# Two chains of the delta rule: the order of emission charges more for the three DVE steps of a chunk, in three of four pairs of heads

## The chip, the cores and the metric

One core of a Trainium2 chip. The metric is the device time of one execution in microseconds. An execution runs five engines with a queue each: PE (TensorE, matmuls; its weight loads are listed as PEld), DVE (VectorE), ACT (ScalarE), POOL (GpSimd) and SP (SyncE, which issues DMAs here). Each engine takes its queue in order, and an instruction waits on semaphores for the results of others.

## The reference

One layer of a hybrid encoder for a prompt of 2048 rows and a sample of 32, with 1024 columns, cut to what matters here:

```python
hp = layer_norm(x_prompt, ln0_g, ln0_b)
qa, ka, va, za, qkv_b, zb, a_b, b_b, gate_a, gate_b = split_projection(x @ w_in)
oa = chunk_band_attention(qa, ka, va, rel_bias)          # branch A, 8 heads of 64
c = silu(causal_conv(xp, conv_w, t))                     # branch B, 8 heads of 64
ob, s_new = gated_delta_rule(qb, kb, vb, g, beta, s_prev)
mix = sigmoid(gate_a) * ya + sigmoid(gate_b) * yb
y = layer_norm(ALPHA * x + mix @ w_out, ln_g, ln_b)
```

The delta rule works in chunks of 64 rows. Within a chunk everything can be prepared ahead (a triangular system per chunk and head); between chunks a state of 64 x 64 per head is handed on, which is a chain:

```python
def step(s, blk_in):
    q_c, k_c, u_c, w_c, gc_c, qk_c = blk_in
    v_new = u_c - w_c @ s
    o_c = (q_c * exp(gc_c)) @ s + qk_c @ v_new
    s = s * exp(g_last) + k_dec.T @ v_new
    return s, o_c
```

## The kernel before

The prompt is worked in two halves of 1024 rows. In each half come the input projection (jobs of 128 output columns, three passes of fp16 matmuls over 8 slices of the depth, into the PSUM tile `pj`), branch B (`phase_b`: convolution, gates, triangular systems, chains), then branch A (`phase_a`: scores, softmax, values). After both halves come the merge of the branches and the output projection. The jobs of the projection feed the branches, and those of the two merge gates feed nothing before the end and serve as filling: `all_jobs` lists them, with six gate jobs (`TAIL`) between branch B's jobs and branch A's.

The heads of branch B go in four pairs (`NP`), and a pair's 16 chunks of a half in two blocks of 8. A block's way is: `system` forms the chunk matrices (tiles `k_bd`, `qk_bd`, `p_c`), `solve` and `substitute` solve the triangular systems on DVE (31 pairs of `sys_t` and `sys_u`), `inverse` turns the result into `u_bd`, and `chain` runs through the chunks. Two banks (`x_banks = places(2)`) allow two chains at a time. In the second half the sample makes one more block, whose four chunks are the four pairs. Each chunk of a chain has three matmuls on PE into the tile `x`, each followed by a step on DVE that the next matmul needs:

- `x<-state,k_bd`, then DVE's `r` (a scalar_tensor_tensor)
- `x<-r,u_bd`, then DVE's `vn` (a tensor_scalar)
- `x<-vn,kd_bd`, then DVE's `state` (a scalar_tensor_tensor), for the next chunk

Two more matmuls per chunk, `o<-state,q_bd` and `o<-vn,qk_bd`, give the output, which ACT copies into `v_t`; `tail` scales and stores it.

The order of all queues is made by a planner in the program itself. Every piece of work is a generator (a `Stream`) with a clock of its own; `Flow.run` always resumes the stream whose clock is lowest, and each instruction that it emits moves its clock, and that of its engine, by a price (`Engine.price`, `Flow.spend`). For an instruction of DVE that reads PSUM the price is 0.125 us and 1/960 us per element, and 0.2 us more for coming from another engine (`HOP`); a matmul of fp32 into 64 columns has 128/600 us. The prices set the order of emission alone; on the chip nothing but queues and semaphores decides when something runs. The lines that charge:

```python
t = s.clock + (HOP_SAME if s.last == key else HOP)
t = max(t, self.busy.get(key, 0.0)) + cost
self.busy[key] = s.clock = t
```

All instructions are issued through one wrapper, line 259 of the kernel before (261 of the one after), so rows are told apart by their tiles.

Of the kernel before, what the change touches and what calls it, by code (L numbers as in the profile page):

```python
# [29 lines left out]
NP = NH // 2  # L30
# [18 lines left out]
NPAR, NSIDE = 4, 3  # L49
HEAD, TAIL = [2, 3], [6, 6]  # L50
AHEAD = 100.0
SPREAD = 20.0
HOP_PE, HOP, HOP_SAME = 0.1, 0.2, 0.12

# [213 lines left out]
def trunk(ctx: ExitStack, tc: tile.TileContext, x_p, x_s, cache_k, cache_v, st_conv, st_gdn,  # L268
# [4 lines left out]
    flow = Flow()  # L273
# [6 lines left out]
    def dma(dst, src, eng=nc.sync):  # L280

        eng.dma_start(dst, src)  # L282
        size = 2 if dst.dtype == F16 else 4
        n = size
        for k in dst.shape:
            n *= k

        n = max(n, n // (size * dst.shape[-1]) * 768)
        return flow.transfer("SP" if eng is nc.sync else "S", n)
# [153 lines left out]
    def spread():  # L443

        for h in range(NH):
            dma(ext_dram[h][:], ext_row[h:h + 1, :].to_broadcast([P, 768]))
            yield flow.cur.clock + SPREAD

# [327 lines left out]
    def phase_b(half):  # L776
# [518 lines left out]
        def outputs(m, x, os_, vc=None, end=None):  # L1295


            PE.matmul(os_, m, x, start=vc is None, stop=vc is not None)
            yield
            if vc is not None:  # L1300
                S.copy(out=vc, in_=os_)
                if end:
                    end.done()

        def chain(some):
            for k in some:
                yield k.ready
                xn = yield from x_banks.take()
                sc, v_t = k.sc, k.v_t
                xs, ys, ds_ = (xb[xn][:, i * HD:(i + 1) * HD] for i in range(3))  # L1310
                os_ = ob_[xn][:, 0:HD]
                for c in range(k.nch):
                    st = k.state[c]
                    vc = v_t[:, c if k.p is None else c % 4 * 2 + c // 4, :]
                    PE.matmul(xs, k.kb[:, c, :], st, start=True, stop=True)
                    yield
                    r = bp.tile([P, HD], F32, tag=f"r{xn}", bufs=2, name="r")
                    V.scalar_tensor_tensor(out=r[:], in0=xs, scalar=k.negc[:, c:c + 1], in1=vc, op0=ALU.mult, op1=ALU.add)
                    yield
                    PE.matmul(ys, k.ub[:, c, :], r[:], start=True, stop=True)  # L1320
                    flow.start(outputs(k.qb[:, c, :], st, os_))
                    yield
                    vn = bp.tile([P, HD], F32, tag=f"vn{xn}", bufs=2, name="vn")
                    V.tensor_scalar(out=vn[:], in0=ys, scalar1=sc[:, 1, c:c + 1], scalar2=None, op0=ALU.mult)
                    yield
                    PE.matmul(ds_, k.kdb[:, c, :], vn[:], start=True, stop=True)
                    flow.start(outputs(k.qkb[:, c, :], vn[:], os_, vc, k.out if c == k.nch - 1 else None))
                    V.scalar_tensor_tensor(out=st, in0=st, scalar=sc[:, 3, c:c + 1], in1=ds_, op0=ALU.mult, op1=ALU.add)
                    yield
                yield k.out  # L1330
                x_banks.back(xn)
                par_slots.back(k.par)
                side_slots.back(k.sn)
                u_slots.back(k.un)
                flow.start(tail(k))
# [84 lines left out]
        for some in blocks + ([[sample]] if last else []):  # L1420
            flow.start(chain(some))
# [795 lines left out]
    for half in range(2):  # L2217
# [12 lines left out]
        if half == 0:  # L2230
            flow.start(build_h(1, ap, 4), flow.cur.clock + AHEAD)
        if half == 0:
# [62 lines left out]
```

## Time and profile before

| | us |
|---|---|
| median of 3 runs | 2121.21 |
| lowest and highest run | 2118.57, 2124.31 |
| the profiled execution | 2124.96 |
| its span, first to last instruction | 2123.1 |
| PE busy in the span | 1994.4 |
| DVE busy | 1534.2 |
| ACT busy | 978.7 |
| POOL busy | 634.3 |

The span is what the rows below lie in; the time of an execution also has what lies around it. Busy time of PE counts a matmul from its start to a modelled end, so that matmuls which follow each other overlap in the records. Idle time is put down to what released the instruction behind it.

### The profile page before, as it was taken

The page shows a single profiled execution, that of the slowest core. Times are in us where ns is not written, and L with a number is a line of the kernel's source. Part 1 is how long each engine was busy: PE and PEld are TensorE (multiplying, and loading weights), DVE is VectorE, ACT ScalarE, POOL GpSimd, SP SyncE. Part 2 cuts the span into 40 slices and gives each one's busy share as a digit, 9 for nine tenths or more (in the row PEclk, how much of TensorE's full clock was granted, in tenths as well). Part 3 has the DMA queues.
Part 4 walks back from the last instruction along what each step waited for, and adds up shares of the span by engine and source line. Part 5 has one row for each costly group of instructions (what it writes and reads, how often), then busy time and mean ns, then how long its engine had stood idle before and what let it go on. Part 6 is the DMA issues. An engine that isn't in the chain of part 4 may idle for free. (4 is left out here: it accounts for less than half of the span.)

```text
span 2123.1 us, 41363 instructions
## 1 busy us (share of the span) xinstructions
PE 1994.4 (94%) x15098; PEld 1422.5 (67%) x15098; DVE 1534.2 (72%) x4660; ACT 978.7 (46%) x2098; POOL 634.3 (30%) x708
## 2 busy tenths in 40 slices
PE   4999898999999999999899999999999988999998
PEld 4454665666465656666666676767776777988896
DVE  7689989884277768779898987347657667766676
ACT  5655544443465667564444443346656652111110
POOL 6243333232322122333233232310110223443343
PEclk9999999899999999999999999999999999999999
DMA  3223232222423233222223233332322435443331
GB/s 120 75 84 102 76 88 78 67 79 82 122 67 120 82 93 99 70 73 76 58 70 94 62 86 85 99 100 72 92 77 67 138 120 191 128 123 103 116 107 61
DMA packets 197719, 196.49 MB, mean 93 GB/s; under 512 B 79622, under 2 KB 147570, under 8 KB 197516
## 3 DMA queue, kind: packets, MB, share of 16 engines
q1 hardware_dynamic: 197516, 193.85, 30.9%
q8 instruction: 119, 1.95, 0.4%
q14 instruction: 84, 0.69, 0.1%
HBM read 135.91 MB, written 50.53 MB: 88 GB/s over the span
## 5 line engine op out<-in xcount | busy, mean ns | idle before, releaser
L259 PE MATMUL pj<-hi,whi 128*128 128x512 f16 (+2 forms) x1992 | 650.7, 342 | 8.6 <-POOL whi L259 3.0
L259 PE MATMUL pj<-hi,wlo 128*128 128x512 f16 (+2 forms) x1952 | 640.8, 341 | 0.4 <-POOL wlo L259 0.4
L259 PEld LDWEIGHTS <-whi 128*128 128x128 f16 x3984 | 416.0, 106 | 217.5 <-issue 11.2
L259 PE MATMUL pj<-lo,whi 128*128 128x512 f16 (+2 forms) x1992 | 461.9, 340 | 0.0
L259 POOL TENSOR_TENSOR wlo<-wraw,whi 128x512 f16<-128x512 f32 x192 | 228.6, 1193 | 630.1 <-ACT whi L259 345.1
L259 PEld LDWEIGHTS <-wlo 128*128 128x128 f16 x1952 | 205.5, 105 | 108.5 <-issue 8.9
L259 ACT CAST mh<-sg 128x256 fp32r<-128x256 f32 x64 | 25.9, 407 | 276.1 <-DVE sg L259 276.0
L259 DVE TENSOR_TENSOR sys_u<-sys_u,sys_t 128x60 f32<-128x60 f32 (+24 forms) x527 | 135.7, 258 | 18.2
L259 PE MATMUL a<-ghi,whi 128*128 128x256 f32 (+1 forms) x512 | 134.8, 293 | 7.1 <-DVE sg L259 6.8
L259 ACT ACTIVATE wraw<-wraw,w_scale 128x1024 f32<-128x1024 f32 (+1 forms) x98 | 111.4, 1137 | 59.2 <-DVE w_scale L259 57.1
L259 ACT CAST ph<-b 128x512 f16<-128x512 f32 (+2 forms) x224 | 92.6, 422 | 92.7 <-PE b L259 86.1
L259 PE MATMUL a<-ghi,wlo 128*128 128x256 f32 (+1 forms) x512 | 131.9, 287 | 0.0
L259 ACT CAST whi<-wraw 128x512 f16<-128x512 f32 (+1 forms) x196 | 119.4, 611 | 27.1 <-PE pj L259 24.2
L259 DVE TENSOR_TENSOR pl<-b,ph 128x512 f16<-128x512 f32 (+2 forms) x224 | 107.6, 484 | 28.9 <-ACT ph L259 28.0
L259 DVE TENSOR_TENSOR sys_t<-sys_u,sys_p 128x54 f32<-128x54 f32 (+21 forms) x459 | 123.6, 269 | 4.0
L259 ACT ACTIVATE sb<-sb,mx,unit 128x640 f32<-128x640 f32 (+4 forms) x128 | 109.0, 852 | 25.5 <-DVE mx L259 25.1
L259 DVE SCALAR_TENSOR_TENSOR acc<-raw,cwT,acc 128x512 f32<-128x512 f32 x144 | 113.2, 786 | 8.4 <-ACT acc L259 7.4
L259 POOL TENSOR_TENSOR w_scale<-w_scale,mhalf 128x1 f32<-128x1 f32 x49 | 31.0, 633 | 288.0 <-DVE w_scale L259 230.1
L259 PEld LDWEIGHTS a<-ghi,whi 128*128 128x128 f32 x512 | 99.3, 194 | 8.8 <-DVE sg L259 7.9
L259 PE MATMUL b<-ident,sb 128*128 128x128 f32 x560 | 98.8, 276 | 2.9 <-ACT tmp L259 0.6
L259 ACT COPY v_t<-o 128x64 f32<-128x64 f32 x132 | 27.5, 209 | 158.3 <-PE o L259 121.5
L259 PEld LDWEIGHTS a<-ghi,wlo 128*128 128x128 f32 x512 | 98.9, 193 | 0.4 <-DVE wlo L259 0.2
(350 smaller groups left out, 4238.9 us busy)
## 6 DMA issues: line engine op xcount, KB each, us to landing
wraw<-in_w_in SPq DMA_DIRECT2D x192, 256.0 KB
sg<-sig SPq DMA_DIRECT2D x112, 128.0 KB
sig<-sig SPq DMA_DIRECT2D x44, 256.0 KB
sys_p<-sol_p SPq DMA_DIRECT2D x17, 512.0 KB
x<-in_x_p SPq DMA_DIRECT2D x16, 512.0 KB
xt<-in_x_p SPq DMA_DIRECT2D x16, 512.0 KB
out_y_p<-xt SPq DMA_DIRECT2D x16, 512.0 KB
glo<-g SPq DMA_DIRECT2D x14, 512.0 KB
```

Source lines behind the costliest of these rows:

```text
L259: r = f(*a, **k)
```

## The change

A constant is added, and in `chain` the clock of the stream is moved on by it after each of the three DVE steps, for pairs 0, 1 and 2 (`k.p in range(NP - 1)`); for pair 3 and for the sample (`k.p` is `None`) it is 0. The clock of DVE is not moved, only that of the chain: other streams may emit their work in the time between.

```diff
 AHEAD = 100.0
+
+SLACK = 0.4
...
                 sc, v_t = k.sc, k.v_t
+                slack = SLACK if k.p in range(NP - 1) else 0.0
...
                     V.scalar_tensor_tensor(out=r[:], in0=xs, scalar=k.negc[:, c:c + 1], in1=vc, op0=ALU.mult, op1=ALU.add)
+                    flow.cur.clock += slack
                     yield
...
                     V.tensor_scalar(out=vn[:], in0=ys, scalar1=sc[:, 1, c:c + 1], scalar2=None, op0=ALU.mult)
+                    flow.cur.clock += slack
                     yield
...
                     V.scalar_tensor_tensor(out=st, in0=st, scalar=sc[:, 3, c:c + 1], in1=ds_, op0=ALU.mult, op1=ALU.add)
+                    flow.cur.clock += slack
                     yield
```

The instructions are the same in number on every engine. Their order differs from the first chain on, at 209 us of the trace before. Two places on PE and one on DVE show how.

PE, first half, third chunk of pair 0's first block, from the matmul that takes r to the one that takes vn. `pj` rows are projections, `LDWEIGHTS` rows the loads of their weights. Before:

```order
L259 MATMUL x<-r,u_bd_629 128x64
L259 LDWEIGHTS whi
L259 MATMUL pj<-lo_151,whi 128x512
L259 MATMUL o<-state,q_bd_617 128x64
L259 LDWEIGHTS whi
L259 MATMUL pj<-lo_151,whi 128x512
L259 MATMUL x<-vn,kd_bd_623 128x64
```

Now:

```order
L261 MATMUL x<-r,u_bd_629 128x64
L261 LDWEIGHTS whi
L261 MATMUL pj<-hi_152,whi 128x512
L261 MATMUL o<-state,q_bd_617 128x64
L261 LDWEIGHTS wlo
L261 MATMUL pj<-hi_152,wlo 128x512
L261 LDWEIGHTS whi
L261 MATMUL pj<-hi_152,whi 128x512
L261 LDWEIGHTS wlo
L261 MATMUL pj<-hi_152,wlo 128x512
L261 MATMUL x<-vn,kd_bd_623 128x64
```

Between the two chain matmuls stand four projections where there were two.

PE, second half, fifth chunk of pair 0's first block, from the matmul that takes vn to the next chunk's first. `b<-qk,k_bd` rows are the chunk matrices of a later block. Before:

```order
L259 MATMUL x<-vn,kd_bd_10329 128x64
L259 MATMUL b<-qk_11407,k_bd_10313 128x128
L259 LDWEIGHTS wlo
L259 MATMUL pj<-hi_9644,wlo 128x512
L259 MATMUL o<-vn,qk_bd_10315 128x64
L259 MATMUL x<-state,k_bd_10307 128x64
```

Now:

```order
L261 MATMUL x<-vn,kd_bd_10298 128x64
L261 MATMUL b<-qk_11407,k_bd_10282 128x128
L261 LDWEIGHTS whi
L261 MATMUL pj<-hi_9940,whi 128x272
L261 MATMUL o<-vn,qk_bd_10284 128x64
L261 MATMUL b<-qk_11407,k_bd_10282 128x128
L261 LDWEIGHTS wlo
L261 MATMUL pj<-hi_9940,wlo 128x272
L261 MATMUL x<-state,k_bd_10276 128x64
```

One projection and one matmul of a chunk matrix have come between, and the place now falls among projections of 272 columns.

DVE, first half, the third chunk again, from r to state. `v_t` and `sys` rows belong to the preparation of later blocks. Before:

```order
L259 SCALAR_TENSOR_TENSOR r<-x,negc,v_t_654 128x64
L259 SCALAR_TENSOR_TENSOR qk_2258<-e,acc 128x512
L259 TENSOR_TENSOR v_t_656<-b,sc 64x2x2x64
L259 TENSOR_SCALAR vn<-x,sc 128x64
L259 TENSOR_TENSOR v_t_656<-b,swap 64x2x2x64 x2
L259 SCALAR_TENSOR_TENSOR state<-state,sc,x 128x64
```

Now:

```order
L261 SCALAR_TENSOR_TENSOR r<-x,negc,v_t_654 128x64
L261 TENSOR_TENSOR v_t_656<-b,swap 64x2x2x64 x2
L261 TENSOR_SCALAR sys_t<-sys_p,sys_u 128x31
L261 TENSOR_TENSOR sys_u<-sys_u,sys_t 128x31
L261 TENSOR_SCALAR vn<-x,sc 128x64
L261 TENSOR_TENSOR v_t_656<-b,sc 64x2x2x64
L261 TENSOR_SCALAR sys_t<-sys_p,sys_u 128x30
L261 TENSOR_TENSOR sys_u<-sys_u,sys_t 128x30
L261 SCALAR_TENSOR_TENSOR state<-state,sc,x 128x64
```

More of DVE's other work stands between the steps of a chunk too.

## Rows read from the trace of the kernel before

**Rows 1.** The page: busy time of each engine, share of the span.
```profile
PE 1994.4 (94%) x15098; PEld 1422.5 (67%) x15098; DVE 1534.2 (72%) x4660; ACT 978.7 (46%) x2098; POOL 634.3 (30%) x708
```

**Rows 2.** Busy time by stretch; the first row names the columns.
```profile
core 0: us, PE busy (x) PEld busy (x) DVE busy (x) ACT busy (x) POOL busy (x), PEclk, DMA share, GB/s
209.00:465.00 256.00, 236.57 (x1744) 161.02 (x1741) 224.50 (x803) 117.75 (x250) 80.24 (x102) 0.95 0.29 81
...
465.00:525.00 60.00, 57.68 (x460) 39.58 (x454) 31.16 (x124) 23.41 (x53) 15.59 (x14) 1.00 0.27 79
525.00:589.00 64.00, 64.00 (x304) 29.56 (x303) 17.98 (x62) 27.98 (x43) 23.59 (x24) 1.00 0.38 116
...
1016.00:1274.00 258.00, 236.71 (x2020) 176.63 (x2020) 227.12 (x796) 114.31 (x264) 80.71 (x111) 0.99 0.29 75
```

**Rows 3.** Waits of weight loads, 209 to 465 us: total, times, longest.
```profile
PEld x L259 <- DVE vn L259: 15.4, 23, 1.8
PEld x L259 <- DVE r L259: 14.8, 26, 1.3
PEld x L259 <- DVE state L259: 8.9, 15, 1.9
```

**Rows 4.** The same from 1016 to 1274 us.
```profile
PEld x L259 <- DVE vn L259: 15.6, 27, 1.5
PEld x L259 <- DVE r L259: 14.9, 27, 1.8
PEld x L259 <- DVE state L259: 10.7, 19, 2.6
```

**Rows 5.** The same in the last pair: 465 to 525, 1274 to 1353 us.
```profile
PEld x L259 <- DVE r L259: 6.4, 14, 0.8
PEld x L259 <- DVE vn L259: 2.1, 3, 1.5
...
PEld x L259 <- DVE r L259: 4.1, 15, 0.5
PEld x L259 <- DVE vn L259: 2.9, 10, 1.0
PEld x L259 <- DVE state L259: 1.8, 8, 0.3
```

**Rows 6.** Timeline around 363 us: start, duration, what, [idle before and its releaser].
```profile
362.08 1.03 PE L259 MATMUL pj<-lo,whi 128*128 128x512 f16 x4
362.15 1.23 POOL L259 TENSOR_TENSOR wlo<-wraw,whi 128x512 f16<-128x512 f32 x1 [2.75 <-ACT whi L259]
362.29 1.16 DVE L259 TENSOR_TENSOR sys_t<-sys_u,sys_p 128x50 f32<-128x50 f32 x1
...
363.61 0.28 DVE L259 SCALAR_TENSOR_TENSOR r<-x,negc,v_t 128x64 f32<-128x64 f32 x1
363.81 0.20 DVE L259 TENSOR_SCALAR gz<-gnw,w_inv 128x1 f32<-128x1 f32 x1
363.94 0.30 PEld L259 LDWEIGHTS x<-r,u_bd 128*128 128x128 f32 x2 [1.33 <-DVE r L259]
363.94 0.43 PE L259 MATMUL x<-r,u_bd 128*128 128x64 f32 x2 [0.84 <-DVE r L259]
```

**Rows 7.** Tile sys_t: count, shortest/median/longest in ns, first and last start.
```profile
L259 DVE TENSOR_TENSOR sys_t<-sys_u,sys_p x459: 153/215/1221, 146.7 to 1323.7; 128x54 f32<-128x54 f32 x32, 128x48 f32<-128x48 f32 x17, 128x63 f32<-128x63 f32 x17, 128x72 f32<-128x72 f32 x17
```

**Rows 8.** Timeline at 1060 us, PE: two projections of 272 columns.
```profile
1060.08 0.28 PE L259 MATMUL pj<-hi,whi 128*128 128x272 f16 x1
1060.19 0.28 PE L259 MATMUL pj<-hi,wlo 128*128 128x272 f16 x1
```

**Rows 9.** Busy time from 300 to 350 us, columns as in rows 2.
```profile
300.00:350.00 50.00, 45.23 (x344) 30.33 (x343) 46.15 (x165) 24.37 (x52) 19.22 (x24) 1.00 0.35 103
```

**Rows 10.** Tile kst, 520 to 700 us: the first score matmuls.
```profile
L259 PE MATMUL a<-kst,qd x47: 219/299/379, 589.1 to 699.5; 128*128 128x320 f16 x31, 128*128 128x128 f16 x4, 128*128 128x256 f16 x4, 128*128 128x384 f16 x4
```

## The prediction

> **What bounds the kernel now.** I read the page's busy times first: PE is busy for 1994.4 of 2123.1 us [rows 1], so whatever shortens the kernel has to take idle time out of PE's queue. Then the busy times by stretch [rows 2], with cuts at the places that the change touches: each half of the sequence has one stretch in which the chains of the delta rule run, 209 to 525 us in the first half and 1016 to 1352 us in the second, and the chains of the first three pairs of heads end at 465 and at 1274 us. In the stretches of those three pairs PE is busy for 236.57 of 256 us and for 236.71 of 258 us, while behind the chains, from 525 us to the first score matmul at 589.1 us [rows 10], it has no idle time at all. Last, what the weight loads wait for in these stretches [rows 3, 4]: nearly all of it is the three results that DVE hands back to a chain, r, vn and state. 64 waits take 39.1 us in the first half (15.4 + 14.8 + 8.9) and 73 take 41.2 us in the second (15.6 + 14.9 + 10.7): 137 waits among 288 steps (2 halves x 6 blocks x 8 chunks x 3 steps), 80.3 us.
>
> One wait in full [rows 6]: DVE's sys_t, an instruction of 0.22 us in the median [rows 7], takes 1.16 us while POOL's wlo subtraction of 1.23 us runs; r, next but one behind it in DVE's queue, starts at 363.61 and takes 0.28 us; the weight load of the chain's next matmul has stood for 1.33 us and goes at 363.94. The last of the four projection matmuls before it started at about 362.73 (four from 362.08 on, 0.215 apart, from 1.03 us for all with 0.38 for one), so PE's next place was free at 362.94, and 1.0 us was lost. PE's queue is in order: the projections behind the waiting matmul needed nothing from DVE and stood too.
>
> What the 137 waits cost lies between two ends. The weight loads' 80.3 us are too much, since a load may stand while the matmul before it still runs (1.33 against 1.0 above). PE's idle time in the two stretches, 19.4 + 21.3 = 40.7 us [rows 2], is too little, since a projection's record lasts 0.38 us where the next one starts 0.215 us after it. I take the middle, 61 us.
>
> **The change, part by part.** No instruction is added or dropped; each engine has as many as before, DMAs included. What changes is the clock of a chain in the emission: three times 0.4 us per chunk, for 96 chunks (2 x 6 x 8).
>
> *Distance on PE.* The chain's next matmul comes later in PE's queue, and more of the projections stand before it. I counted, block by block, the projection matmuls between the block's first and last chain matmul in the two orders. First half: 96, 95, 97, 111, 94, 65 (558 in all) become 112, 89, 113, 152, 99, 92 (657). Second half: 116, 167, 116, 107, 107, 132 (745) become 159, 169, 148, 161, 164, 148 (949). A projection of 512 columns occupies 0.215 us and one of 272 columns 0.115 us [rows 6, 8]; the first half has the former in its stretch, the second a mixture of about a third to two thirds, 0.15 us. So 99 more matmuls are 21.3 us over 144 steps, 0.15 us per step, and 204 more are 30.6 us, 0.21 us per step. This is less than the 0.4 us that is charged, because the charge counts only where the clock of the emission was not already held by a busy PE or DVE.
>
> *What a wait loses by it.* A wait longer than the added distance becomes shorter by that distance; a step that did not wait gains nothing. 64 x 0.15 + 73 x 0.21 = 9.6 + 15.3 = 25 us. The bounds: nothing, if DVE comes later by the same amount (first rival), and 137 x 0.4 = 55 us, if every waiting step got the whole charge. I take 25 us, since it is counted from the order itself.
>
> *The chains' length.* In the first half the last chain matmul stands behind projection 1381 before and 1456 now. The 75 projections that it falls back by were there anyway: the first score matmul of the attention stands in both orders behind projection 1664, and PE is busy for 64.00 of 64 us up to it [rows 2, 10]. Price 0, covered by the projections from 1456 to 1664; without that cover it would be 75 x 0.215 = 16 us. In the second half the last one stands at 4478 before and at 4479 now: 0.
>
> *DVE.* Its work stays the same, 224.50 us in 256 and 227.12 us in 258 [rows 2], 88%. For the forecast the same work must fit into 256 - 10 and 258 - 15 us, 91% and 93%. Its busiest 50 us have 46.15 us, 92% [rows 9], so this is about the most that this kernel has shown, and it is why I don't take more than 25 us. The first half has some relief: its chains end 75 projections later, in a stretch where DVE is busy for 31.16 of 60 and 17.98 of 64 us [rows 2].
>
> *The clock of TensorE.* It was granted at 0.95 and 0.99 in the two stretches [rows 2]; at half the full rate for a tenth of 256 us that is up to 12.8 us, and 2.6 us in the second. [...]
>
> *The queues of SP, ACT and POOL.* Their instructions move along with the blocks (a block's output scaling, its DMAs, the next system's inputs). ACT and POOL have over half of each stretch free [rows 2]: 0.
>
> Sum: -25 us. The profiled execution took 2124.96 us, the median of the runs is 2121.21 us; taken from the median this gives **2096 us**. A change under 0.3%, 6 us, can't be told from none here.
>
> **The rivals.** *The waits are DVE's backlog* (0.15): then the distance on PE is used up. What the emission charges for r, 0.125 us + 64/960, is 0.19 us; the record has 0.28 us, and the next instruction on DVE starts 0.20 us after r [rows 6]. If the charge is as good as right, the waits come from what stands before r on DVE, and DVE, already 88% busy, merely spends the same time elsewhere. For it: sys_t above, and the 92%. Against it: a delay of 0.9 us behind one POOL instruction is a matter of moments, and that is what distance covers. It gives 2121 us, within 6.
> [...]
>
> *The waits pass to the last pair* (0.12), which gets no extra time. In the second half its first block now starts at projection 4271 where it was 4320, right behind the end of the third pair's chain (4268, before 4220); the pause of 100 projections in which DVE could catch up is gone. The last pair and the sample have 108 steps and wait 17.3 us by [rows 5], 0.16 us per step; the first three pairs wait 80.3 / 288 = 0.28 us. If theirs rose to that, 108 x 0.12 = 13 us would be lost, and with nothing gained before, by the first rival, it ends at 2134 us, slower. It decides where DVE still has a backlog when the last pair starts. Against it: in the first half that pair has DVE at half load.
>
> *All waits go and the clock stays up* (0.08): 61 + 15 us, 2045 us. It needs DVE at more than 100% of the shortened second stretch (227 us in 258 - 41), so only a part of it can come.
>
> That the change does nothing is out: nearly every row of PE's order from the first chain on has another neighbour.
>
> **How the numbers follow.** The forecast has 0.65: with the third rival, faster has 0.73, the same 0.15, slower 0.12. The range goes from 2066 us (the 55 us of the upper bound) to 2127 us (the upper edge of the first rival): it leaves out the second and the third rival, 0.20.
>
> **What would show it.** Right: the waits of x's weight loads on r, vn and state in the two stretches fall from 80 us to about 50 us, the chains of the first half end later against the projections but the first scores come some 10 us earlier than 589 us, and the score stage of the second half some 25 us earlier; DVE's share in the stretches rises to 91% or more. Wrong: as many waits with DVE's share unchanged (first rival), or the last pair's 17 us doubled (second). An earlier end of the chains with the gain lost again in the attention would contradict the sum altogether.

## The result, and the profile after

The changed kernel takes **2128.53 us** (median of 17 runs, 2122.77 to 2133.03) where the kernel before takes 2120.11 us on the same chips (17 runs, 2117.17 to 2125.50): ratio 1.0039, interval 1.0030 to 1.0048. It is slower by 8.4 us; 2096 was forecast, 2127 was the upper end of the range, and slower had 0.12. The profiled execution took 2131.02 us, its span is 2128.8 us.

PE's busy time on the page is to the tenth what it was [rows 1], so by the page the difference of the two spans, 5.7 us, is idle time of PE. Busy time is no fixed quantity, though: the same matmuls are busy for 1970.9 us in e18 below.

```profile
PE 1994.4 (94%) x15098; PEld 1430.6 (67%) x15098; DVE 1533.2 (72%) x4660; ACT 980.7 (46%) x2098; POOL 633.0 (30%) x708
```

The busy times by stretch, with the same cuts and columns as [rows 2]:

```profile
209.00:465.00 256.00, 233.56 (x1670) 157.76 (x1667) 207.61 (x737) 118.38 (x243) 79.07 (x103) 0.92 0.31 79
465.00:525.00 60.00, 57.88 (x476) 40.62 (x475) 40.16 (x164) 24.92 (x57) 16.57 (x15) 1.00 0.32 91
525.00:589.00 64.00, 58.93 (x314) 32.57 (x313) 21.85 (x80) 22.17 (x40) 20.39 (x20) 0.97 0.28 86
1016.00:1274.00 258.00, 235.79 (x2055) 180.86 (x2054) 225.82 (x780) 116.26 (x264) 78.09 (x109) 0.96 0.29 77
```

Three things stand against the forecast. In the first stretch PE is busy for 3.0 us less, and DVE, which was to come to 91%, has fallen from 224.50 to 207.61 us (81%): the chains advance more slowly, and the third pair's ends at 501 us where it ended at 465. Of these 36 us, the 116 more projections that now stand in front of that end make 25 (at 0.215 us). The granted clock there is 0.92 where it was 0.95, and 0.96 in the second half where it was 0.99. And from 525 to 589 us, where PE had no idle time at all, it now lacks 5 us.

The waits of x's weight loads, and DVE's own for a load, in the two stretches of [rows 3, 4]; first 209 to 465 us:

```profile
PEld x L261 <- DVE r L261: 13.8, 14, 5.7
PEld x L261 <- DVE vn L261: 12.6, 14, 4.1
DVE sys_t L261 <- DMA sys_p<-sol_p: 10.5, 3, 4.9
PEld x L261 <- DVE state L261: 6.3, 12, 1.0
```

and 1016 to 1274 us:

```profile
PEld x L261 <- DVE vn L261: 15.4, 18, 3.4
PEld x L261 <- DVE r L261: 13.5, 15, 3.2
DVE sys_t L261 <- DMA sys_p<-sol_p: 7.0, 4, 3.2
PEld x L261 <- DVE state L261: 5.1, 13, 1.0
```

There are fewer waits, 40 and 46 where there were 64 and 73, with a sum of 32.7 + 34.0 = 66.7 us instead of 80.3. But these stretches hold all 144 steps of the three pairs in the kernel before, and only 120 and 132 in the changed one. Over the whole of these chains (209 to 501 and 1027 to 1293 us) it has 51 waits of 38.7 us and 50 of 36.2, 74.9 us in all: in the first half the sum has not fallen at all (39.1 before), since the longest last 5.7 and 4.1 us where the longest before was 1.9. And there is a wait that the prediction does not know: DVE's `sys_t`, the first step of a triangular system, stands for the load of its input `sys_p`, 10.5 and 7.0 us. Before, there were none from 209 to 600 us, and from 1017 to 1430 us

```profile
DVE sys_t L259 <- DMA sys_p<-sol_p: 2.6, 2, 2.3
```

The first score matmul of the first half comes at 598.9 us, not some 10 us before 589.1 [rows 10] but 9.8 us behind it:

```profile
L261 PE MATMUL a<-kst,qd x48: 219/299/379, 598.9 to 708.0; 128*128 128x320 f16 x32, 128*128 128x128 f16 x4, 128*128 128x256 f16 x4, 128*128 128x384 f16 x4
```

In this pair of profiles the first half loses about 10 us. The first score matmul of the second half comes at 1430.5 us where it came at 1424.1, 6.4 us behind: between them 3.4 us are won back. A single profile is good to 6 or 8 us here: e2 below, whose first half has the order of the kernel before, has its first scores at 583.2 us (granted clock from 209 to 465 us 0.99), and e1, whose first half has that of the changed kernel, at 591.1 us (0.96). In this second pair the loss is 8 us, and the clock falls by 0.03 as in the first.

**The first place of the loss**, in the timeline of the changed kernel (SP's, DVE's and PE's rows of the same 15 us, one engine after the other):

```profile
363.36 1.29 SPq L284 DMA_DIRECT2D g<-gb  x2
364.82 0.57 SPq L284 DMA_DIRECT2D sys_p<-sol_p  x1
...
372.46 0.21 DVE L261 TENSOR_TENSOR sys_u<-sys_u,sys_t 128x48 f32<-128x48 f32 x1
376.98 0.24 DVE L261 TENSOR_SCALAR sys_t<-sys_p,sys_u 128x31 f32<-128x31 f32 x1 [4.31 <-DMA sys_p<-sol_p]
377.25 0.19 DVE L261 TENSOR_TENSOR sys_u<-sys_u,sys_t 128x31 f32<-128x31 f32 x1
377.48 0.28 DVE L261 SCALAR_TENSOR_TENSOR r<-x,negc,v_t 128x64 f32<-128x64 f32 x1
...
377.82 0.69 PE L261 MATMUL x<-r,u_bd 128*128 128x64 f32 x2 [5.58 <-DVE r L261]
378.30 0.63 PE L261 MATMUL o<-state,q_bd 128*128 128x64 f32 x2
378.73 0.63 PE L261 MATMUL pj<-hi,whi 128*128 128x512 f16 x1
379.15 0.63 PE L261 MATMUL pj<-hi,wlo 128*128 128x512 f16 x1
```

SP issues the load at 364.82, DVE can use it at 376.98, 12.2 us later. DVE's queue is in order: `r` stands behind `sys_t`, PE's matmul behind `r`, the projections behind the matmul, and PE is idle for 5.58 us. Behind the stop the projections follow each other by 0.43 us where they had 0.215 [rows 6]: the clock is at half (granted 0.50 from 378 to 381 us). The same happens at 275.6 us (DVE 4.87 us, PE 3.83).

In the kernel before, the systems of this stretch had more time. One of them:

```profile
335.27 0.59 SPq L282 DMA_DIRECT2D sys_p<-sol_p  x1
...
351.79 0.24 DVE L259 TENSOR_SCALAR sys_t<-sys_p,sys_u 128x31 f32<-128x31 f32 x1
```

From the issue of the load to the first `sys_t`, the five systems whose loads are issued between 256 and 458 us took 16.15, 10.14, 16.52, 15.46 and 11.83 us, and now take 10.82, 12.22, 12.16, 12.06 and 11.02. Where DVE stood for it, the load had taken 10.8 to 12.2 us; three of the five had left it 3 to 6 us more than that. The planner prices it at 0.2 + 0.5 + 0.6 + 512 KB / 200 KB per us + 1.6, 5.5 us where no other transfer is booked in front of it, and emits `sys_t` as soon as that is over. By the code (this part is argued, not measured), `sys_t` comes later than that where DVE's clock in the emission is ahead; the extra 0.4 us of the chains changes which stream goes first, and the short price shows.

**The second place**, in the changed kernel's timeline from 557 us (PE's, ACT's and SP's rows in order of time, others left out):

```profile
557.18 1.02 SPq L284 DMA_DIRECT2D wraw<-in_w_in  x2
...
557.55 1.89 PE L261 MATMUL pj<-lo,whi 128*128 128x512 f16 x8
...
559.53 1.06 ACT L261 ACTIVATE whi<-wraw 128x1024 f16<-128x1024 f32 x1 [5.91 <-issue]
...
560.73 0.38 PE L261 MATMUL b<-w_sq,tiny 128*128 128x1 f32 x2 [1.29 <-ACT whi L261]
...
562.23 1.15 ACT L261 ACTIVATE wraw<-wraw,w_scale 128x1024 f32<-128x1024 f32 x1 [1.55 <-DVE w_scale L261]
...
563.93 1.26 ACT L261 ACTIVATE vf<-pj,w_inv 128x512 f32<-128x512 f32 x2
...
564.66 0.58 PE L261 MATMUL pj<-hi,whi 128*128 128x512 f16 x1 [3.55 <-ACT vf L261]
565.04 0.63 PE L261 MATMUL pj<-hi,wlo 128*128 128x512 f16 x1
```

PE stops for 1.3 and 3.6 us, and goes on at half clock. The first stop is for `whi`, the next weights in fp16, which ACT begins only at 559.53; what held it, the row doesn't show. The second is for `vf`, the eviction of branch A's first job out of `pj`. Its target belongs to phase A, and the program closes phase B's pools and opens phase A only when the last block of the chains has been stored. The chains now end 75 projections later, so both evictions of that job are emitted together at projection 1520, when both `pj` tiles are full, and behind the scaling of the next weights in ACT's queue. Before, the first was emitted at projection 1497, and PE did not stop.

### The profile page after: what moved, and what is told of

The parts are those of the page before. It is cut to its first block, busy times and chain, and to the rows that moved or that the text cites. A ratio compares the mean times of both kernels' runs of the same rounds, so it can differ in the third digit from the quotient of the medians.

```text
span 2128.8 us, 41379 instructions
## 1 busy us (share of the span) xinstructions
PE 1994.4 (94%) x15098; PEld 1430.6 (67%) x15098; DVE 1533.2 (72%) x4660; ACT 980.7 (46%) x2098; POOL 633.0 (30%) x708
## 5 line engine op out<-in xcount | busy, mean ns | idle before, releaser
L261 DVE TENSOR_TENSOR sys_t<-sys_u,sys_p 128x60 f32<-128x60 f32 (+21 forms) x459 | 118.5, 258 | 4.9
L261 ACT COPY v_t<-o 128x64 f32<-128x64 f32 x132 | 27.8, 211 | 172.5 <-PE o L261 140.0
L261 DVE CUSTOM_DVE_ANT_0 sb<-a,bias 128x320 f32<-128x320 f32 (+4 forms) x128 | 61.4, 486 | 52.2 <-PE a L261 51.4
```

The source lines that it names most:

```text
L261: r = f(*a, **k)
```

## The experiments

Two theories stood at first. **A**: the loss is DVE standing for the load of `sys_p`, and the half clock behind it. **B**: the extra time on the three steps costs by itself. After the second group came **C**: the later end of the chains has a price too. All ratios are to the kernel before, run on the same chip.

**Which half loses?**

```diff
-                slack = SLACK if k.p in range(NP - 1) else 0.0
+                slack = SLACK if half == 0 and k.p in range(NP - 1) else 0.0    # e1; half == 1 in e2
```

> The extra charge in the first half alone. Theory A (the loss comes from DVE standing for the load of a triangular system, sys_p, which the new order puts closer in front of its first sys_t; the two long waits of 4 to 5 us lie in the first half, and PE's clock is lower behind them): as slow as the change, 2126 to 2131 us, granted clock 0.975 or lower. Theory B (any stretch with chain matmuls spread over more projections costs, because PE is interrupted more often): half of the loss, 2123 to 2126 us.

> The extra charge in the second half alone. Theory A: the profile of the change gains some 4 us from 1017 us on, so 2114 to 2119 us, clock about that of the kernel before. Theory B: half of the loss, 2123 to 2126 us.

Measured: e1 2130.26 us, 1.0057 (1.0037 to 1.0078); e2 2113.45 us, 0.9979 (0.9964 to 0.9995). The first half alone makes the whole loss and more; the second half is a gain of 4.5 us (1 to 8 by its interval).

**The load of sys_p charged 5 us more, in both halves.**

```diff
+LATE = 5.0
...
-                yield dma(sys_p[:].rearrange("p j i -> p (j i)"),
+                yield LATE + dma(sys_p[:].rearrange("p j i -> p (j i)"),
```

e3 is the changed kernel with it, e4 the kernel before with it.

> The change, and the order of emission counts 5 us more for the landing of sys_p before the first sys_t. Theory A: DVE's waits for sys_p (10.5 us in the first half, 7.0 us in the second) go to under 4 us together, the granted clock comes back to 0.98 or more, and what the distance saves shows: 2100 to 2116 us. Theory B: the clock stays at 0.975 and the time at 2122 to 2130 us.

> The kernel before, with the same 5 us for the landing of sys_p. Theory A: it waits for sys_p for 2.6 us only, and 2 x 2.5 us more through PE, so 2112 to 2120 us; what it gains is less than what the same edit gains on the change (8 us or more against 0 to 8). Theory B: 2117 to 2123 us.

Measured: e3 2131.04 us, 1.0051 (1.0033 to 1.0070); e4 2124.91 us, 1.0025 (1.0012 to 1.0038). By the total, theory A has missed. By stages it has not: no `sys_t` waits for its load in e3, and its first scores come at 580.9 us, 10 us ahead of e1's. Both kernels lose behind the first scores of the second half: from there to the end e3 takes 708 us and e4 707, the kernel before 699 and the changed one 698. LATE moves the end of that half's chains from projection 4478 to about 4600; that this is the reason was not tested. So the next runs have LATE in the first half only.

**The late load in the first half.**

```diff
-                yield LATE + dma(sys_p[:].rearrange("p j i -> p (j i)"),
+                yield (LATE if half == 0 else 0.0) + dma(sys_p[:].rearrange("p j i -> p (j i)"),
```

> The extra 0.4 us in the first half only, as in e1, but there the load of sys_p is charged 5 us more before its stream may emit DVE's first sys_t; the second half is that of the kernel before, unlike in e3. Theory A (what e1 lost is DVE standing for the load of sys_p in the first half, and the low clock behind those stops; the extra time on the three steps itself does no harm): the first half comes as in e3, first score matmul about 8 us before that of the kernel before instead of 2 to 10 us behind it, no wait of sys_t for the load over 1 us between 209 and 600 us, and a time of 2107 to 2117 us where e1 had 2130. Theory B (the extra time itself costs, by more interruptions of PE, wherever sys_p comes): 2124 to 2132 us, like e1.

> The change in both halves, with the load of sys_p charged 5 us more in the first half only. Theory A: the first half of e8 and the second half of e2 (which was 6 us faster than before), so 2102 to 2112 us, faster than both kernels; what e3 lost was its second half, where the late load moved the end of the chains from projection 4479 to 4607. Theory B: 2118 to 2128 us.

> The kernel before, with the load of sys_p charged 5 us more in the first half only: the control for e8, without any extra time on the steps of a chunk. Theory A: the kernel before has hardly a wait of DVE for sys_p in the first half, so little is to be had from their absence alone; but e4's first half came 6 us earlier: 2110 to 2119 us. If e8 is under this one, the extra time pays in the first half once the load is covered; if they are the same, it gives nothing there; if e8 is over it by 6 us or more, theory B holds in part.

> The extra 0.4 us in the second half only, as in e2, and the load of sys_p charged 5 us more in the first half only. By e2 (6 us) and the first half of e4 (6 us): 2102 to 2112 us by either theory. Against e7 it tells what the extra time is worth in the first half with the load covered.

| | extra time in | us | ratio, interval |
|---|---|---|---|
| e8 | first half | 2119.23 | 1.0005 (0.9994 to 1.0015) |
| e7 | both | 2115.03 | 0.9976 (0.9960 to 0.9991) |
| e9 | none | 2123.36 | 1.0018 (1.0006 to 1.0029) |
| e10 | second half | 2117.87 | 0.9999 (0.9986 to 1.0011) |

With the load covered, the extra time in the first half goes from 1.0057 to 1.0005, 11 us, and the whole change from 1.0039 to 0.9976, 13 us. Theory B falls: with LATE in place the extra time is no loss in the first half. e8 is 3 us under e9 and e7 5 us under e10, each pair with intervals that overlap, so a gain is likely but not clear of noise. It is smaller than A said (all four lie over their ranges, by 2, 3, 4 and 6 us): here LATE costs 4 us by itself (e9). The waits of e8 from 209 to 465 us have what the changed kernel should have had, no `sys_t` among them, and 28.6 us in 44 waits (125 steps) instead of 32.7 in 40 (120 steps), the longest 2.2:

```profile
PEld x L262 <- DVE vn L262: 11.8, 18, 1.7
PEld x L262 <- DVE r L262: 9.9, 14, 2.2
PEld x L262 <- DVE state L262: 6.9, 12, 1.2
```

The stop in front of phase A is still in e8, from 525 to 589 us:

```profile
PE pj L262 <- ACT vf L262: 4.1, 1, 4.1
PEld b L262 <- ACT whi L262: 3.7, 5, 1.8
```

**The chains' end: one gate job more in front of phase A.**

```diff
-HEAD, TAIL = [2, 3], [6, 6]
+HEAD, TAIL = [2, 3], [7, 6]
```

48 projections that need nothing of branch A then stand behind the chains of the first half. e11 is e7 with it, e12 the changed kernel, e13 the kernel before. e5 is the changed kernel with SLACK 0.05, for the effect of another order as such.

> As e7 (the change in both halves, the load of sys_p charged 5 us more in the first half), and one gate job more between branch B's jobs and branch A's in the first half (TAIL [7, 6] for [6, 6]): 48 projections more that need nothing of branch A stand behind the chains. Theory C (the chains' later end has a price too: phase A opens only when the last block of phase B has been stored, and with the chains ending 75 to 83 projections later PE stops 5 to 6 us before projection 1520, for w_sq and for the eviction into vf, and goes on at half clock): that stop is gone, 5 to 9 us are gained on e7 (0.9976 of the kernel before there), so 2103 to 2111 us, about 0.993 to 0.996. Rival D (the stop is made up for later, or the gate job is missed as filling at the end of the half): as e7 or slower, 2113 to 2122 us.

> The changed kernel with TAIL [7, 6] and nothing else: the two stops for sys_p stay, the stop before projection 1520 goes. Theory C: 5 to 9 us under the changed kernel (2128.5 us, 1.0039), so 2118 to 2125 us, 0.9995 to 1.002. Rival D: 2126 to 2133 us.

> The kernel before with TAIL [7, 6]: the control. It has no such stop, so theory C gives it nothing, 2116 to 2123 us; a gain of 5 us or more here would say that the gate job pays in itself, a loss of 5 us or more that it is missed at the end of the half.

> The changed kernel with SLACK 0.05 in place of 0.4: an order that differs from that of the kernel before in many places, with hardly any added distance. It shows what a shuffled order alone does. By theory A with C the loss needs the later loads of sys_p and the later end of the chains; where neither has moved it stays within 6 us of the kernel before, 2114 to 2126 us. If it is slower by as much as the changed kernel, the loss is one of the order at large and not of the two places named.

| | us | ratio, interval |
|---|---|---|
| e11 | 2108.09 | 0.9941 (0.9923 to 0.9960) |
| e12 | 2121.88 | 1.0014 (0.9998 to 1.0031) |
| e13 | 2127.89 | 1.0035 (1.0020 to 1.0051) |
| e5 | 2114.79 | 0.9973 (0.9957 to 0.9990) |

The same edit takes 7 us from e7 (0.9976 to 0.9941) and 5 us from the changed kernel (1.0039 to 1.0014), and costs the kernel before 7 us (5 us over its range). What it costs there was not followed up; that it helps only where the chains end late is theory C's sign. `PE pj <- ACT vf` is gone from the waits of e11 and e12. e5 bounds what may be read from such steps: its order has 13 and 29 projections more between the chains' matmuls where the changed kernel has 99 and 204, no stop in front of phase A, and it is 6 us faster than the kernel before. A shifted order as such is worth that much, so a single step of 3 to 7 us shows its cause only together with the wait that goes or comes with it.

**What is the extra time worth, with both places covered?** e14, e15 and e16 are e11 with the extra time in the second half, in the first half, and in none.

> e11 with the extra 0.4 us in the second half only; LATE and TAIL stay as in e11, so both places that cost time in the first half are covered. Against e11 it shows what the extra time is worth in the first half by itself. By the prediction's term for that half (99 projections more, 9.6 us) it is 9 to 10 us slower than e11, about 2117 us (0.9985 of the kernel before). Rival: the distance gives nothing there, 2105 to 2111 us like e11.

> e11 with the extra 0.4 us in the first half only. Against e11 it shows what the extra time is worth in the second half. By the prediction's term (204 projections more, 15.3 us) about 2123 us (1.002); by what e2 and e7 gave (4 to 6 us) 2111 to 2115 us (0.996 to 0.998).

> The kernel before with LATE in the first half and TAIL [7, 6], without any extra time: the control for e11, e14 and e15. By the prediction's two terms 25 us over e11, about 2133 us; by e9 and e13 (4 us and 8 us over the kernel before, if they add) 2127 to 2133 us. If it is at 2112 us or less, the gain of e11 comes from LATE and TAIL and the extra time gives nothing.

| | extra time in | us | ratio, interval |
|---|---|---|---|
| e16 | none | 2121.24 | 1.0010 (1.0001 to 1.0020) |
| e14 | second half | 2120.59 | 0.9998 (0.9985 to 1.0010) |
| e15 | first half | 2113.19 | 0.9974 (0.9961 to 0.9986) |
| e11 | both | 2108.09 | 0.9941 (0.9923 to 0.9960) |

In the first half it is worth 0.0036 (e16 to e15) and 0.0057 (e14 to e11), 8 and 12 us, 10 in the mean: the prediction's term of 9.6. In the second half it is worth 0.0012 and 0.0033, 3 and 7 us, the former within the noise, where the term was 15.3. LATE and TAIL by themselves give nothing (e16, 6 us under its range: their costs in e9 and e13 don't add).

Three more pairs differ by TAIL alone. Where the chains of the first half end late (projection 1464) it gains 7 us again (e8 to e15). Where they end at projection 1422 it gives 2 us (e9 to e16) and nothing (e10 to e14); there PE's wait for `vf` was short from the start (0.2 us in e4, whose first half has the same order). With the three pairs above that is 5, 7 and 7 us gained with a late end, and 2, 0 and -7 without one, as theory C has it.

**The load of sys_p in the second half.** e18 is e11 with 3 us there (5 us in the first half); e19 is e18 with the extra time in the first half only.

```diff
-                yield (LATE if half == 0 else 0.0) + dma(sys_p[:].rearrange("p j i -> p (j i)"),
+                yield (LATE if half == 0 else 3.0) + dma(sys_p[:].rearrange("p j i -> p (j i)"),
```

> e11 with the load of sys_p charged 3 us more in the second half too (5 us in the first); TAIL stays [7, 6], and the chains of the second half end at projection 4522 instead of 4479. If DVE's waits for sys_p in the second half (5.0 us in e11) and the low clock behind them are what the second half lacks, 2096 to 2104 us (0.989 to 0.9925), provided that the later end makes no new stop in front of phase A; if the second half's distance gives no more than it did, 2105 to 2112 us, like e11.

> e18 with the extra 0.4 us in the first half only: against e18 it shows what the extra time is worth in the second half with the load of sys_p covered there. By the prediction's term (15.3 us) it is 15 us over e18; by what e11 against e15 gave (7 us for the ratios 0.9941 and 0.9974) 5 to 8 us over it. The late load alone should change little here, since the second half without the extra time has only 1.6 us of such waits: 2109 to 2116 us, like e15.

Measured: e18 **2099.49 us**, 0.9925 (0.9901 to 0.9949); e19 2118.47 us, 1.0004 (0.9991 to 1.0017). Their difference is 0.0079, 17 us, against the prediction's 15.3. Only the extra time differs between them, but the control is a poor one: e19 is 6 us slower than e15 and 2 us over its range, so the late load costs something there without the extra time. With it, e18 is not clearly faster than e11 (0.0016 with intervals of about 0.002 on either side), so that covering the load pays in this half is not shown. From e15, the better control, e18 is 0.0049 or 10 us away. e18 is the fastest kernel of the study, 18.5 us under the kernel before and, by the ratios (0.9925 against 1.0039), 24 under the changed one. The waits of e18, 209 to 465 us and then 1003 to 1261 us:

```profile
PEld x L262 <- DVE vn L262: 11.8, 18, 1.7
PEld x L262 <- DVE r L262: 9.2, 13, 2.2
PEld x L262 <- DVE state L262: 6.8, 12, 1.2
...
PEld x L262 <- DVE vn L262: 13.4, 18, 2.0
PEld x L262 <- DVE r L262: 7.3, 15, 1.1
PEld x L262 <- DVE state L262: 5.4, 12, 1.2
```

and its busy times in these stretches, columns as in [rows 2]:

```profile
209.00:465.00 256.00, 241.04 (x1798) 161.44 (x1795) 220.96 (x791) 125.22 (x256) 84.50 (x109) 0.98 0.31 87
1003.00:1261.00 258.00, 238.32 (x2125) 182.79 (x2124) 233.90 (x820) 120.09 (x274) 84.22 (x116) 0.99 0.30 81
```

88 waits of 53.9 us remain of 137 of 80.3 [rows 3, 4]; over the whole of the three pairs' chains, 216 to 494 and 1013 to 1268 us (with the last pair's first steps), it is 92 waits of 55.6 us. No `sys_t` waits for its load, and the clock is at 0.98 and 0.99. PE issues 1798 matmuls in the first stretch where the kernel before issued 1744 and the changed one 1670. Its page, with a span of 2095.3 us, has

```profile
PE 1970.9 (94%) x15098; PEld 1415.3 (68%) x15098; DVE 1532.3 (73%) x4660; ACT 979.4 (47%) x2098; POOL 634.5 (30%) x708
```

One more kernel, e17, had TAIL [7, 7] beside e18's loads (2108.40 us, 0.995). It computes other rows of y than the reference, for a reason that was not found, so nothing is concluded from it.

## Why the prediction was wrong

*What bounds the kernel: PE's queue, rightly, but not its idle time on the page.* e18's span is 27.8 us shorter than that of the kernel before; 23.5 of these are busy time of PE (1994.4 to 1970.9) and only 4.3 idle time. A projection's record lasts 0.38 us where the next one starts after 0.215, and 0.63 us at half clock where it starts after 0.43, so the first part of each wait, and all of the half clock, is booked as busy. The waits of x's weight loads are the right place only together with what stands in front of them: in the changed kernel they fell by 5 us and the time rose by 8, in e18 they fell by 25 us and the time by 18.5.

*Distance on PE, and what a wait loses by it: right in kind, in size for the first half only, and not in this kernel.* Predicted were 9.6 and 15.3 us. With the side effects covered the extra time gives 8 to 12 us in the first half (e16 to e15, e14 to e11). In the second it gives between 3 us (e16 to e14) and 17 (e19 to e18), by the control that is taken, so its size there stays open. From the control without extra time to e18 it is 18 us (e16 to e18) of the 25, and 54 to 56 us of waits are left where about 50 were said. Part of this agreement may be luck, since another order alone gave 6 us (e5). In the changed kernel itself, costs that stood at 0 in the sum ate the gain.

*"The queues of SP, ACT and POOL: 0". This step failed, and it is the main one.* It looked at how busy these engines are, not at how much time a DMA on them has between its issue and its use. The chains' extra time moved the emission of the loads of `sys_p` and of their first use nearer to each other, from up to 16.5 us to 11 or 12, what the load takes. DVE stood for it, with a chain step behind. Price in the first half, by LATE: 11 us (e1 to e8) to 13 us (changed kernel to e7), which is more than e5's 6 us. In the second half DVE stood 7.0 us for the load, with a price that is not shown. What could have warned was in the trace: `sys_t` waiting 2.6 us for `sys_p` in the second half of the kernel before, and the 10 to 12 us from issue to use in the timeline.

*"The chains' length: price 0". This failed too.* The cover was counted right, 208 projections between the chains' end (1456) and the first scores (1664). But branch A's first job stands among them and can't be evicted before phase A is open, which waits for the chains' last block. The true cover was the 64 projections up to 1520, less the time that the block's tail takes. Price by TAIL: 5, 7 and 7 us in three pairs, with a stop of 4.8 us in the trace that goes with it. In the second half, where the end moved by one projection, 0 was right.

*The clock of TensorE: bounded on one side only.* The prediction took 15 us as a possible gain and nothing as a loss. Behind the stops for `sys_p` and `vf` PE went on at half clock, and the granted clock fell by 0.03 from 209 to 465, from 525 to 589 and from 1016 to 1274 us; the kernel before had half clock too (granted 0.50 from 370 to 380 us, projections 0.43 us apart, behind waits of at most 1.6 us), so not every fall has such a stop. Every execution has its mean granted clock in the results: 0.972 to 0.978 in the 17 of the changed kernel, 0.979 to 0.989 in all of the kernel before that ran beside the experiments. Among the 17, one with 0.001 less is some 1.3 us longer (2122.77 us at 0.978, 2133.03 at 0.972). The means, 0.975 and 0.983, are then 10 us apart, by this estimate as much as the whole loss. That it is no cost beside those of the stops but the form that part of them takes is the author's reading and was not shown: e1 and e8, with DVE's waits for `sys_p` in the first half and without them, have the same mean (0.979) and lie 11 us apart. e18 has the clock of the kernel before (0.983), so its gain is none of the clock's.

*DVE's work: right*, 1533.2 us against 1534.2 [rows 1]. In e18 it reaches 91% in the second stretch (233.90 of 258 us), the least that the forecast asked for; in the first, 86%.

*The rivals.* The first (DVE's backlog) is not what happened: the distance did pay once the loads and the chains' end were covered. The second foresaw 2134 us by more waits in the last pair: its three results waited 10.6 us from 465 to 543 us (7.5 + 1.6 + 1.5) and 13.2 us from 1274 to 1360 us (5.5 + 4.4 + 3.3) where [rows 5] had 17.3 in all. 6.5 us more there are half of the 13 that it charged, and in stretches that are longer by the chains' later end; the loss of the first half had arisen before. The rival that would have been right, a transfer whose lead is used up by the shift, was not among them.

## What to carry to other kernels

When a change moves the order of emission, list the loads whose first use stands near their issue, with the lead that each has in the trace and the time that it takes; a load at the edge of its lead is a term of the sum, even where its queue is idle most of the time (here DVE stood 10.5 us for such loads in a stretch with a DMA share of 0.31). A later end of one stage is free only up to the first instruction that the next stage's opening holds back, not up to the next stage's main work (here projection 1520, not 1664). A local gain that a change buries can be brought out by covering its side effects one at a time, with a control for each cover: here the same charge goes from 0.4% slower to 0.75% faster, while two of the three covers without it give nothing (e16). And in a kernel whose order a planner makes, run one change that shifts the order and hardly anything else: what it moves, here 0.3%, is what a single step must exceed, or else the wait that it removes must be seen to go. Compare the clocks of the executions along with their times.

## What the runs showed that was not expected

The 512 KB load of `sys_p`, each of four groups of 32 partitions taking the same data, was used 10.2 to 12.2 us after its issue in the eight places of the changed kernel where DVE stood for it (9.8 the shortest of 17 in the kernel before), about twice the 5.5 us that the planner charges. Stops of PE of 3.8 and 5.6 us were followed by projections at 0.43 us instead of 0.215. And a cover can cost where it is not needed: one gate job moved forward gives 7 us in e11 and takes 7 us in e13.
